# First sweep of a bidirectional GLA + latent-attention layer: chunk products in float32 from whole operands, the two directions' scores on the two halves of the rows

## The chip, the cores and the metric

The kernel runs on one core of a Trainium2 chip. Its time is the device time of one execution in microseconds. Three runs of the kernel before took 1295.48, 1295.50 and 1295.51 us; the median is 1295.5 us.

The engines of the core are named as in the profile: PE multiplies matrices (PEld is its loading of the stationary operand, "the weights"), DVE, ACT and POOL work elementwise, SP issues DMAs. PE writes to PSUM only.

## What is computed

One encoder layer on 2048 tokens of width 1024: one input projection, two groups of mixers beside each other (gated linear attention, GLA, and latent softmax attention, MLA), one output projection, LayerNorm. The change lies in the GLA alone, for which the reference does this, once forwards and once backwards over the sequence (in chunks of 64; four heads, keys of width 64, values of width 128):

```python
b = jnp.cumsum(gc, axis=3)              # running log decay inside a chunk
q_dec = qc * jnp.exp(b)
k_dec = kc * jnp.exp(-b)
k_tail = kc * jnp.exp(b_last - b)
attn = jnp.where(mask, jnp.einsum('nbhtd,nbhsd->nbhts', q_dec, k_dec), 0.0)
o_intra = jnp.einsum('nbhts,nbhsv->nbhtv', attn, vc)
def step(state, inp):
    qd, kt, vv, bl = inp
    o = jnp.einsum('bhtd,bhdv->bhtv', qd, state)
    state = state * jnp.exp(bl[:, :, 0, :])[..., None] + jnp.einsum('bhsd,bhsv->bhdv', kt, vv)
    return state, o
```

All of it is float32.

## The kernel before

**Two sweeps and an attention.** The sequence is cut into 16 chunks of 128 tokens. The first sweep (`sweep_a`) goes through them from the last (c = 15, i = 0) to the first (c = 0, i = 15). For each it projects x onto the GLA columns (`products`: three groups of columns, tile `ipa`) and the gate (`gate_products`, tile `ipg`), forms the decays (`ga_z`, `ga_sums`), and computes the chunk's own part of the GLA in both directions plus the running state of the backward direction. The second sweep (`sweep_c`) goes forwards, reads what the first has stored to DRAM, and makes the keys and queries of the MLA; then come the attention and the output.

**Both directions in one tile.** The 128 partitions of `qd` and `kd` hold 64 key dimensions of the forward direction and, below them, 64 of the backward direction. So a head's scores are two products over 64 rows each: rows 0 to 63 give the forward scores, rows 64 to 127 the backward ones.

**Split products.** Products that need more than one pass of precision are made from high and low parts in the type float32r: `hi` (L370, a copy on ACT into float32r) and `lo` (L376, the difference, on DVE or POOL). `mm3` (L424 to L426) is high x high, high x low, low x high. In the first sweep this is done for

- the scores `Ap` (`ga_intra`): `kd` is split into `kh` and `kl`; `qd` is split into `qbh` and `qbl`, which are laid out block-diagonally (`[P, H, 2, P]`, zeros outside the blocks, set once by POOL at the start), so that one product of 128 rows gives both directions, 256 columns wide. Twelve products for a chunk;
- the state's update `Up` (`ga_state`): `kd` transposed, split into `kth`, `ktl`, against `VV`, which holds the values' high and low part beside each other. A 256-column product and a 128-column one for each head: eight;
- the output of the chunk `Op` (`ga_av`): the masked scores `At` split into `Ah`, `Al`, against `VV`. Eight.

Results that are 256 columns wide hold two halves that ACT and DVE then add: `Us` (ACT copy L1047, DVE add L1049, scaled by the decay `cw` on POOL at L1051) and `oi` (L1029, L1031).

**Order.** Chunks 15 to 12 (i = 0 to 3) follow the string `ORDER_A`, whose entries name a step of a generator (`ga_q`, `ga_k`, ...; a step ends at a `yield`); `in_order` ties the instructions of each engine to this order. From i = 4 the steps of a chunk are placed between the products of the next one by `STEPS_A`: `intra` after the last products of group 1, `state` after the fourth k-step of group 2, `av` in the gate's products. Within this the framework's scheduler orders each engine's instructions. PE works through them in order.

**State.** `Sb` (rows 64 to 127) is the backward state. `ga_bst` stores `Sb` times one decay and multiplies `Sb` by another (POOL, L1072 and L1076); the last step of `ga_state` adds `Us` (POOL, L1057). From i = 3 `ga_bst` runs inside `ga_state`; before that `ORDER_A` places it.

**Buffers.** `gp` is a PSUM pool of two buffers of two banks each, used in turn by `Ap`, `Up`, `Op`. `g1` and `wa` hold the sweep's tiles in SBUF; when the sweep ends the weights of the second sweep (`wm`, `wz`) are loaded where the first sweep's were.

Of the kernel before, what the change touches and what calls it, by code (L numbers as in the profile page):

```python
# [18 lines left out]
P = 128  # L19
# [4 lines left out]
H = 4  # L24
# [58 lines left out]
    lo=(11.99, 11.22, 11.21, 12.62, 11.98, 11.51, 10.87, 10.63),  # L83
    pv=(12.35, 12.1, 11.89, 12.65, 12.27, 12.25, 12.14, 11.45),
# [20 lines left out]
    lo=(15.35, 16.07, 20.38, 20.41, 24.45, 25.82, 33.5, 36.25),  # L105
    pv=(16.29, 16.53, 21.45, 24.62, 26.22, 30.32, 41.89, 43.83),
# [82 lines left out]
    lo=(-0.5, 0.357),  # L189
# [79 lines left out]
    lo=(-0.452, -1.813),  # L269
# [65 lines left out]
    lo=(-0.124, 0.045),  # L335
# [24 lines left out]
class K:  # L360
# [262 lines left out]
    def sweep_a(self):  # L623
        tc, nc, ins, cp = self.tc, self.nc, self.ins, self.cp
        with ExitStack() as ctx:
            wp = ctx.enter_context(tc.tile_pool(name="wa", bufs=1, reuse_waits="tile"))
            xp, ip, tr, gp = self.xab, self.ip, self.tr, self.gp
# [3 lines left out]
            mask = wp.tile([P, P], I32, name="mask")  # L631
            rmask = wp.tile([P, H, P], F32, name="rmask")
            wg = wp.tile([98, H, P], F32R, name="wg")
            lrs = [wp.tile([P, 98], F32R, name=f"lr{i}") for i in range(2)]
            qbh = [wp.tile([P, H, 2, P], F32R, name=f"qbh{i}") for i in range(1)]
            qbl = [wp.tile([P, H, 2, P], F32R, name=f"qbl{i}") for i in range(1)]
            Sb = wp.tile([P, H, P], F32, name="Sb")
            pos_i = wp.tile([P, NCH], I32, name="pos_i")
            pos_f = wp.tile([P, NCH], F32, name="pos_f")
# [4 lines left out]
            nc.scalar.preload_act_table_set(EXP_LN)  # L644
            for t in lrs:
                nc.vector.memset(t[:, 96:98].bitcast(F32), 1.0)
            for t in qbh + qbl:
                nc.gpsimd.memset(t.bitcast(F32), 0.0)
            nc.vector.memset(Sb, 0.0)

            with tc.tile_pool(name="sta", bufs=1, reuse_waits="tile") as sta:
# [5 lines left out]
                for g, (_, n) in enumerate(A_GROUPS):  # L657
                    k = 0
                    for m in W_PIECES[g]:
# [26 lines left out]
            nc.sync.dma_start(invf, ins["invf"])  # L686
            g1 = ctx.enter_context(tc.tile_pool(name="g1", bufs=1))

            cst = dict(qbh=qbh[0], qbl=qbl[0], Sb=Sb, mask=mask, rmask=rmask, wg=wg, g1=g1, tr=tr, gp=gp)
            rope = self.rope_angles(pos_i, pos_f, invf, hpi)  # L690
            ch = self.ch = [dict(cst, c=NCH - 1 - i, i=i, lr=lrs[i % 2]) for i in range(NCH)]
            self.wa = [(wah[:, k], wal[:, k]) for k in range(NK)]
# [26 lines left out]
            for t in ORDER_A.split():  # L719
                n, i = t.split(".")  # L720
# [6 lines left out]
            for i in range(4, NCH):  # L727
                c = ch[i]["c"]
# [13 lines left out]
            i = NCH - 1  # L742
# [5 lines left out]
                    run("kt", i)  # L748
            self.xlate.append(self.split_x(self.xab, self.xraw, NCH - 2, "xb", "dve", 2))
            run("intra", i)  # L750
            with self.after(ch[i]["Ahi"]):
                self.gate_end(0, g1)
            run("state", i)
            run("av", i)
# [46 lines left out]
        yield  # L801

    def ga_v1(self, d):
        VV = d["VV"] = d["g1"].tile([P, H, 2, P], F32R, tag="VV", name=f"VV_{d['c']}", bufs=2)
        self.hi(VV[:, 0, 0], d["pt", 1][:, 256:384])
        yield
        self.lo(VV[:, 0, 1], d["pt", 1][:, 256:384], VV[:, 0, 0])
        yield

    def ga_v3(self, d):  # L810
        VV, pv = d["VV"], d["pt", 2][:, 0:384].rearrange("p (h d) -> p h d", h=3)
        self.hi(VV[:, 1:4, 0], pv)
        yield
        self.lo(VV[:, 1:4, 1], pv, VV[:, 1:4, 0])
        yield

    def ga_ld(self, i):
# [131 lines left out]
    def ga_q(self, d):  # L949

        nc, c = self.nc, d["c"]
        qbh, qbl = d["qbh"], d["qbl"]
        qT = d["tr"].tile([P, H, P], F32, tag="tr", name=f"qT{c}")
        for h in range(H):
            nc.tensor.transpose(qT[:, h], d["q2"][:, h].rearrange("p a d -> p (a d)"), self.ident)
        yield
        qd = self.t512(d, "qd")
        nc.vector.scalar_tensor_tensor(qd, qT, 0.125, d["E1"], ALU.mult, ALU.mult)
        self.store(c).dma_start(self.qd_s[c], qd.rearrange("p h t -> p (h t)"))
        yield  # L960
        halves = (slice(0, 64), 0), (slice(64, 128), 1)
        for r, j in halves:
            self.hi(qbh[r, :, j], qd[r])
            yield
        for r, j in halves:
            self.lo(qbl[r, :, j], qd[r], qbh[r, :, j])
            yield

    def ga_k(self, d):

        nc, c = self.nc, d["c"]
        kT = d["tr"].tile([P, H, P], F32, tag="tr", name=f"kT{c}")
        for h in range(H):
            nc.tensor.transpose(kT[:, h], d["k2"][:, h].rearrange("p a d -> p (a d)"), self.ident)
        yield
        kd = d["kd"] = self.t512(d, "kd")
        nc.vector.tensor_tensor(kd, kT, d["E2"], ALU.mult)
        yield
        kh = d["kh"] = self.t512(d, "kh", dt=F32R)
        self.hi(kh, kd)  # L980
        yield
        kl = d["kl"] = self.t512(d, "kl", dt=F32R)
        self.lo(kl, kd, kh)
        yield

    def ga_kt(self, d):

        nc, c = self.nc, d["c"]
        kt = d["tr"].tile([P, H, P], F32, tag="tr", name=f"kt{c}")
        for h in range(H):  # L990
            nc.tensor.transpose(kt[:, h], d["kd"][:, h], self.ident)
        yield
        kth = d["kth"] = self.t512(d, "kth", dt=F32R)
        self.hi(kth, kt)
        yield
        ktl = d["ktl"] = self.t512(d, "ktl", dt=F32R)
        self.lo(ktl, kt, kth)
        yield

    def ga_intra(self, d):  # L1000

        nc, c = self.nc, d["c"]
        Ap = d["gp"].tile([P, H, 2, P], F32, tag="gp", name=f"Ap{c}")
        for h in range(H):
            self.mm3(Ap[:, h], d["kh"][:, h], d["kl"][:, h], d["qbh"][:, h], d["qbl"][:, h])
        yield
        At = self.t512(d, "At")
        nc.scalar.activation(At, Ap[:, :, 1], AF.Copy)
        yield
        nc.vector.copy_predicated(At, d["mask"][:, None, :].to_broadcast([P, H, P]), Ap[:, :, 0])  # L1010
        yield
        Ah = d["Ah"] = self.t512(d, "Ah", dt=F32R)
        d["Ahi"] = self.hi(Ah, At)
        yield
        Al = d["Al"] = self.t512(d, "Al", dt=F32R)
        self.lo(Al, At, Ah)
        yield

    def ga_av(self, d):
        nc, c = self.nc, d["c"]  # L1020
        mm = nc.tensor.matmul
        Ah, Al, VV = d["Ah"], d["Al"], d["VV"]
        Op = d["gp"].tile([P, H, 2, P], F32, tag="gp", name=f"Op{c}")
        for h in range(H):
            mm(Op[:, h], Ah[:, h], VV[:, h], start=True, stop=False)
            mm(Op[:, h, 0], Al[:, h], VV[:, h, 0], start=False, stop=True)
        yield
        oi = self.t512(d, "oi", bufs=2)
        nc.scalar.activation(oi, Op[:, :, 1], AF.Copy)  # L1029
        yield  # L1030
        nc.vector.tensor_tensor(oi, Op[:, :, 0], oi, ALU.add)  # L1031
        self.store(c).dma_start(self.oi_s[c], oi.rearrange("p h t -> p (h t)"))
        yield

    def ga_state(self, d):

        nc, c = self.nc, d["c"]
        mm, V, G = nc.tensor.matmul, nc.vector, nc.gpsimd
        kth, ktl, VV, Sb, cw = d["kth"], d["ktl"], d["VV"], d["Sb"], self.cw[:, c]
        lo, up = slice(0, 64), slice(64, 128)  # L1040
        Up = d["gp"].tile([P, H, 2, P], F32, tag="gp", name=f"Up{c}")
        for h in range(H):
            mm(Up[:, h], kth[:, h], VV[:, h], start=True, stop=False)
            mm(Up[:, h, 0], ktl[:, h], VV[:, h, 0], start=False, stop=True)
        yield
        Us = self.t512(d, "Us")
        nc.scalar.activation(Us, Up[:, :, 1], AF.Copy)  # L1047
        yield
        V.tensor_tensor(Us, Up[:, :, 0], Us, ALU.add)  # L1049
        yield  # L1050
        G.tensor_tensor(Us, Us, cw[:, 1, :, None].to_broadcast([P, H, P]), ALU.mult)  # L1051
        self.store(c).dma_start(self.su_s[c][lo], Us.rearrange("p h t -> p (h t)")[lo])
        yield
        if d["i"] > 2:
            yield from self.ga_bst(d)
        if c > 0:
            G.tensor_tensor(Sb[up], Sb[up], Us[up], ALU.add)  # L1057
        yield

    def ga_bst(self, d):  # L1060
# [987 lines left out]
```

## Time and profile before

| | |
|---|---|
| median of three runs | 1295.5 us |
| the profiled execution, its time | 1295.28 us |
| its span, first to last instruction | 1293.4 us |
| mean granted TensorE clock | 0.998 |
| busy over the span: PE, PEld | 1273.7 us, 1127.9 us |
| busy over the span: DVE, ACT, POOL | 962.8, 816.2, 786.1 us |
| DMA | 145.81 MB, mean 113 GB/s |

The profile times each instruction in one execution. The difference between the profiled time and its span, 1.9 us, lies outside the instructions. A PE row gives the time from the start of a product to its modelled end; products overlap in the pipeline, so what a product costs in a stream is the distance from its start to the start of the next. The first sweep's products end at about 358 us; two late gates of chunks 15 and 14 follow up to about 367 us.

### The profile page before, as it was taken

The page shows a single profiled execution, that of the slowest core. Times are in us where ns is not written, and L with a number is a line of the kernel's source. Part 1 is how long each engine was busy: PE and PEld are TensorE (multiplying, and loading weights), DVE is VectorE, ACT ScalarE, POOL GpSimd, SP SyncE. Part 2 cuts the span into 40 slices and gives each one's busy share as a digit, 9 for nine tenths or more (in the row PEclk, how much of TensorE's full clock was granted, in tenths as well). Part 3 has the DMA queues.
Part 4 walks back from the last instruction along what each step waited for, and adds up shares of the span by engine and source line. Part 5 has one row for each costly group of instructions (what it writes and reads, how often), then busy time and mean ns, then how long its engine had stood idle before and what let it go on. Part 6 is the DMA issues. An engine that isn't in the chain of part 4 may idle for free.

```text
span 1293.4 us, 19959 instructions
## 1 busy us (share of the span) xinstructions
PE 1273.7 (98%) x7082; PEld 1127.9 (87%) x7082; DVE 962.8 (74%) x1706; ACT 816.2 (63%) x1334; POOL 786.1 (61%) x494
## 2 busy tenths in 40 slices
PE   8999999999999999999999999999999999999997
PEld 7999999999989999999788888888888888888886
DVE  7966675656675455554898888888888889469997
ACT  7765656566676656665688888888888888511110
POOL 0143333242458666762298888889999999944441
PEclk9999999999999999999999999999999999999999
DMA  8222313132475555665401111122223110366652
GB/s 294 66 92 56 93 53 94 50 86 62 143 261 174 194 197 179 200 208 174 128 1 41 42 42 41 42 58 63 61 72 103 46 41 9 123 214 201 214 193 98
DMA packets 105795, 145.81 MB, mean 113 GB/s; under 512 B 16630, under 2 KB 59262, under 8 KB 105696
## 3 DMA queue, kind: packets, MB, share of 16 engines
q1 hardware_dynamic: 97632, 142.41, 35.3%
q0 software_dynamic: 672, 2.10, 0.4%
q8 instruction: 56, 0.92, 0.3%
q10 hardware_dynamic: 7392, 0.03, 0.3%
q14 instruction: 43, 0.35, 0.1%
HBM read 94.14 MB, written 50.36 MB: 112 GB/s over the span
## 4 chain that ended last, share of the span: by engine, by line
PE 85%; DVE 4%; issue 2%; POOL 2%; ACT 1%; DMA 1%; SPq 0%; DVEq 0%; POOLq 0%
PE pz L1222 6%; PE ipm L1293 5%; PE o L424 4%; PE o L425 4%; PE o L426 4%; PE pS L1554 4%; PE pS L1556 4%; PE pS L1557 4%; PE pS L1555 4%; PE pS L1558 4%; PE ipa L424 4%; PE ipa L426 4%; PE ipa L425 4%; PE ipg L424 2%; PE ipg L425 2%
## 5 line engine op out<-in xcount | busy, mean ns | idle before, releaser
L376 POOL TENSOR_TENSOR pl<-s,ph 128x1024 fp32r<-128x1024 f32 x128 | 306.1, 2409 | 57.5 <-ACT ph L370 53.6
L1576 DVE TENSOR_TENSOR rm<-pS,rm 128x512 f32<-128x512 f32 x210 | 144.8, 690 | 35.8 <-ACT s L1563 30.5
L1563 ACT ACTIVATE s<-pS 128x1024 f32<-128x1024 f32 x128 | 131.3, 1026 | 61.0 <-PE pS L1558 50.8
L1600 DVE TENSOR_TENSOR s<-s,mb 128x1024 f32<-128x1024 f32 x128 | 151.2, 1213 | 9.2 <-PE mb L1594 9.0
L1051 POOL TENSOR_TENSOR Us<-Us,cw 128x512 f32<-128x512 f32 x16 | 20.0, 1247 | 226.3 <-DVE Us L1049 187.8
L370 ACT ACTIVATE ph<-s 128x1024 fp32r<-128x1024 f32 x128 | 135.1, 1057 | 17.4 <-PE o L426 16.6
L1604 ACT ACTIVATE s<-s 128x1024 f32<-128x1024 f32 x128 | 131.4, 1050 | 11.9 <-DVE s L1600 11.9
L424 PE MATMUL ipa<-wah,xah 128*128 128x384 f32 (+1 forms) x384 | 129.0, 336 | 5.4 <-ACT wah L370 5.4
L425 PE MATMUL ipa<-wal,xah 128*128 128x384 f32 (+1 forms) x384 | 124.3, 324 | 0.6 <-DVE wal L376 0.5
L426 PE MATMUL ipa<-wah,xal 128*128 128x384 f32 (+1 forms) x384 | 124.4, 324 | 0.0
L1554 PE MATMUL pS<-qh,ckvT_h 128*128 128x512 f32 x256 | 102.6, 401 | 0.8 <-DVE rm L1576 0.4
L424 PE MATMUL o<-ph,vh 128*128 128x512 f32 x256 | 101.0, 395 | 0.0
L426 PE MATMUL o<-ph,vl 128*128 128x512 f32 x256 | 99.8, 390 | 0.0
L1556 PE MATMUL pS<-qh,ckvT_l 128*128 128x512 f32 x256 | 99.8, 390 | 0.0
L1557 PE MATMUL pS<-rh,krs 128*128 128x512 f32 x256 | 99.8, 390 | 0.0
L1558 PE MATMUL pS<-rl,krs 128*128 128x512 f32 x256 | 99.7, 389 | 0.0
L1555 PE MATMUL pS<-ql,ckvT_h 128*128 128x512 f32 x256 | 99.7, 389 | 0.0
L425 PE MATMUL o<-pl,vh 128*128 128x512 f32 x256 | 99.7, 389 | 0.0
L1627 DVE TENSOR_TENSOR ap<-ap,s 128x512 f32<-128x512 f32 x120 | 83.1, 692 | 2.6 <-ACT s L1604 0.7
L376 POOL TENSOR_TENSOR ol<-of,oh 128x512 fp32r<-128x512 f32 x32 | 42.9, 1342 | 63.8 <-ACT oh L370 63.8
L424 PEld LDWEIGHTS ipa<-wah,xah 128*128 128x128 f32 x384 | 72.8, 190 | 6.6 <-ACT wah L370 5.6
L425 PEld LDWEIGHTS ipa<-wal,xah 128*128 128x128 f32 x384 | 72.8, 190 | 1.8 <-DVE wal L376 1.3
(325 smaller groups left out, 3838.8 us busy)
## 6 DMA issues: line engine op xcount, KB each, us to landing
xcf<-xT_dram SPq DMA_DIRECT2D x16, 512.0 KB, 5.6
xr<-x_dram SPq DMA_DIRECT2D x16, 512.0 KB, 5.5
out_dram<-rr SPq DMA_DIRECT2D x32, 256.0 KB, 2.1
xaf<-xT_dram SPq DMA_DIRECT2D x14, 512.0 KB, 4.2
oib<-oi_s SPq DMA_DIRECT2D x16, 256.0 KB, 4.3
qdb<-qd_s SPq DMA_DIRECT2D x16, 256.0 KB, 5.1
SU<-su_s SPq DMA_DIRECT2D x16, 256.0 KB, 4.9
ub<-u_s SPq DMA_DIRECT2D x16, 256.0 KB, 4.2
```

The costliest lines, as they stand in the source:

```text
L370: return nc.scalar.activation(dst, src, AF.Copy).ins
L376: return e.tensor_tensor(dst, src, hi.bitcast(F32), ALU.subtract).ins
L424: mm(out, ah, bh, start=start, stop=False)
L425: mm(out, ah, bl, start=False, stop=False)
L426: mm(out, al, bh, start=False, stop=stop)
L1554: mm(ps[:, e], kh, qh, start=True, stop=False)
L1555: mm(ps[:, e], kh, ql, start=False, stop=False)
L1556: mm(ps[:, e], kl, qh, start=False, stop=False)
L1557: mm(ps[:, e], kr, rh, start=False, stop=False)
L1558: mm(ps[:, e], kr, rl, start=False, stop=True)
L1576: V.tensor_tensor(d["rm"], src[:, e], d["rm"], ALU.max)
L1600: V.tensor_tensor(s, s, d["mb"][:, None, :].to_broadcast([P, 2, QB]), ALU.subtract)
```

## The change

All three kinds of product are made from whole float32 tiles instead of high and low parts.

- `ga_q` and `ga_k` end with `qd` and `kd`; the tiles `qbh`, `qbl`, `kh`, `kl` and the two memsets go.
- `ga_kt` and `ga_v1`/`ga_v3` copy `kt` and `V` out of PSUM once, on ACT (the copies that were the high parts), as float32; the low parts go.
- `ga_intra`: eight products a chunk, each of 64 rows by 128 columns. The two directions of a head take turns, rows 0 to 63 and rows 64 to 127, and write to different banks of PSUM (`Ap` is now `[P, 2, H, P]`). The masking is as before; `Ah` and `Al` go.
- `ga_av` and `ga_state`: four products of 128 by 128 each. `oi` is one ACT copy; `Us` is one DVE product out of PSUM with the decay `cw`, in place of an ACT copy, a DVE add and a POOL product, and its store to `su_s` is issued behind it. The empty `yield`s keep the state's addition in the fifth step of `ga_state`, behind `ga_bst`.
- `gate_end` of the last chunk waits for the masked scores (`Aset`) instead of their high part (`Ahi`).

On PE the order of the work stays as it was, but for one chunk (i = 4, in which the previous chunk's `kt` transposes and one of its eight score products come before the products of group 1), the place of one `lrT` transpose, and the last chunk, whose `Op` products are no longer spread among those of the late gate.

```diff
-            qbh = [wp.tile([P, H, 2, P], F32R, name=f"qbh{i}") for i in range(1)]
-            qbl = [wp.tile([P, H, 2, P], F32R, name=f"qbl{i}") for i in range(1)]
...
-            for t in qbh + qbl:
-                nc.gpsimd.memset(t.bitcast(F32), 0.0)
...
-            with self.after(ch[i]["Ahi"]):
+            with self.after(ch[i]["Aset"]):
                 self.gate_end(0, g1)
...
     def ga_v1(self, d):
-        VV = d["VV"] = d["g1"].tile([P, H, 2, P], F32R, tag="VV", name=f"VV_{d['c']}", bufs=2)
-        self.hi(VV[:, 0, 0], d["pt", 1][:, 256:384])
-        yield
-        self.lo(VV[:, 0, 1], d["pt", 1][:, 256:384], VV[:, 0, 0])
+        d["V"] = self.t512(d, "V", bufs=2)
+        self.hi(d["V"][:, 0], d["pt", 1][:, 256:384])
         yield
...
     def ga_q(self, d):
...
-        for r, j in halves:
-            self.hi(qbh[r, :, j], qd[r])
-            yield
-        for r, j in halves:
-            self.lo(qbl[r, :, j], qd[r], qbh[r, :, j])
-            yield
...
     def ga_k(self, d):
...
-        kh = d["kh"] = self.t512(d, "kh", dt=F32R)
-        self.hi(kh, kd)
-        yield
-        kl = d["kl"] = self.t512(d, "kl", dt=F32R)
-        self.lo(kl, kd, kh)
-        yield
...
     def ga_kt(self, d):
...
-        kth = d["kth"] = self.t512(d, "kth", dt=F32R)
-        self.hi(kth, kt)
-        yield
-        ktl = d["ktl"] = self.t512(d, "ktl", dt=F32R)
-        self.lo(ktl, kt, kth)
+        d["kt"] = self.t512(d, "kt")
+        self.hi(d["kt"], kt)
         yield
...
     def ga_intra(self, d):
-        Ap = d["gp"].tile([P, H, 2, P], F32, tag="gp", name=f"Ap{c}")
+        Ap = d["gp"].tile([P, 2, H, P], F32, tag="gp", name=f"Ap{c}")
         for h in range(H):
-            self.mm3(Ap[:, h], d["kh"][:, h], d["kl"][:, h], d["qbh"][:, h], d["qbl"][:, h])
-        yield
...
-        Ah = d["Ah"] = self.t512(d, "Ah", dt=F32R)
-        d["Ahi"] = self.hi(Ah, At)
-        yield
-        Al = d["Al"] = self.t512(d, "Al", dt=F32R)
-        self.lo(Al, At, Ah)
+            for j, r in enumerate((slice(0, 64), slice(64, 128))):
+                nc.tensor.matmul(Ap[:, j, h], d["kd"][r, h], d["qd"][r, h], start=True, stop=True)
+        yield
+        At = d["At"] = self.t512(d, "At")
+        nc.scalar.activation(At, Ap[:, 1], AF.Copy)
+        yield
+        d["Aset"] = nc.vector.copy_predicated(At, d["mask"][:, None, :].to_broadcast([P, H, P]), Ap[:, 0]).ins
         yield
...
     def ga_av(self, d):
-            mm(Op[:, h], Ah[:, h], VV[:, h], start=True, stop=False)
-            mm(Op[:, h, 0], Al[:, h], VV[:, h, 0], start=False, stop=True)
+            nc.tensor.matmul(Op[:, h], d["At"][:, h], d["V"][:, h], start=True, stop=True)
         yield
         oi = self.t512(d, "oi", bufs=2)
-        nc.scalar.activation(oi, Op[:, :, 1], AF.Copy)
-        yield
-        nc.vector.tensor_tensor(oi, Op[:, :, 0], oi, ALU.add)
+        nc.scalar.activation(oi, Op, AF.Copy)
...
     def ga_state(self, d):
-            mm(Up[:, h], kth[:, h], VV[:, h], start=True, stop=False)
-            mm(Up[:, h, 0], ktl[:, h], VV[:, h, 0], start=False, stop=True)
+            nc.tensor.matmul(Up[:, h], d["kt"][:, h], d["V"][:, h], start=True, stop=True)
         yield
         Us = self.t512(d, "Us")
-        nc.scalar.activation(Us, Up[:, :, 1], AF.Copy)
-        yield
-        V.tensor_tensor(Us, Up[:, :, 0], Us, ALU.add)
-        yield
-        G.tensor_tensor(Us, Us, cw[:, 1, :, None].to_broadcast([P, H, P]), ALU.mult)
+        nc.vector.tensor_tensor(Us, Up, cw[:, 1, :, None].to_broadcast([P, H, P]), ALU.mult)
         self.store(c).dma_start(self.su_s[c][lo], Us.rearrange("p h t -> p (h t)")[lo])
+        yield
+        yield
         yield
         if d["i"] > 2:
             yield from self.ga_bst(d)
         if c > 0:
-            G.tensor_tensor(Sb[up], Sb[up], Us[up], ALU.add)
+            nc.gpsimd.tensor_tensor(Sb[up], Sb[up], Us[up], ALU.add)
```

More of the change, by code (lines that the diff above doesn't have):

```diff
@@ L687, in sweep_a @@
             g1 = ctx.enter_context(tc.tile_pool(name="g1", bufs=1))
-            cst = dict(qbh=qbh[0], qbl=qbl[0], Sb=Sb, mask=mask, rmask=rmask, wg=wg, g1=g1, tr=tr, gp=gp)
+            cst = dict(Sb=Sb, mask=mask, rmask=rmask, wg=wg, g1=g1, tr=tr, gp=gp)
             rope = self.rope_angles(pos_i, pos_f, invf, hpi)
@@ L803, in ga_v1 @@
     def ga_v1(self, d):
-        VV = d["VV"] = d["g1"].tile([P, H, 2, P], F32R, tag="VV", name=f"VV_{d['c']}", bufs=2)
-        self.hi(VV[:, 0, 0], d["pt", 1][:, 256:384])
-        yield
-        self.lo(VV[:, 0, 1], d["pt", 1][:, 256:384], VV[:, 0, 0])
+        d["V"] = self.t512(d, "V", bufs=2)
+        self.hi(d["V"][:, 0], d["pt", 1][:, 256:384])
         yield
     def ga_v3(self, d):
-        VV, pv = d["VV"], d["pt", 2][:, 0:384].rearrange("p (h d) -> p h d", h=3)
-        self.hi(VV[:, 1:4, 0], pv)
-        yield
-        self.lo(VV[:, 1:4, 1], pv, VV[:, 1:4, 0])
+        self.hi(d["V"][:, 1:4], d["pt", 2][:, 0:384].rearrange("p (h d) -> p h d", h=3))
         yield
@@ L951, in ga_q @@
         nc, c = self.nc, d["c"]
-        qbh, qbl = d["qbh"], d["qbl"]
         qT = d["tr"].tile([P, H, P], F32, tag="tr", name=f"qT{c}")
@@ L956, in ga_q @@
         yield
-        qd = self.t512(d, "qd")
+        qd = d["qd"] = self.t512(d, "qd")
         nc.vector.scalar_tensor_tensor(qd, qT, 0.125, d["E1"], ALU.mult, ALU.mult)
@@ L960, in ga_q @@
         yield
-        halves = (slice(0, 64), 0), (slice(64, 128), 1)
-        for r, j in halves:
-            self.hi(qbh[r, :, j], qd[r])
-            yield
-        for r, j in halves:
-            self.lo(qbl[r, :, j], qd[r], qbh[r, :, j])
-            yield
     def ga_k(self, d):
@@ L1002, in ga_intra @@
         nc, c = self.nc, d["c"]
-        Ap = d["gp"].tile([P, H, 2, P], F32, tag="gp", name=f"Ap{c}")
+        Ap = d["gp"].tile([P, 2, H, P], F32, tag="gp", name=f"Ap{c}")
         for h in range(H):
-            self.mm3(Ap[:, h], d["kh"][:, h], d["kl"][:, h], d["qbh"][:, h], d["qbl"][:, h])
+            for j, r in enumerate((slice(0, 64), slice(64, 128))):
+                nc.tensor.matmul(Ap[:, j, h], d["kd"][r, h], d["qd"][r, h], start=True, stop=True)
         yield
-        At = self.t512(d, "At")
-        nc.scalar.activation(At, Ap[:, :, 1], AF.Copy)
+        At = d["At"] = self.t512(d, "At")
+        nc.scalar.activation(At, Ap[:, 1], AF.Copy)
         yield
-        nc.vector.copy_predicated(At, d["mask"][:, None, :].to_broadcast([P, H, P]), Ap[:, :, 0])
-        yield
-        Ah = d["Ah"] = self.t512(d, "Ah", dt=F32R)
-        d["Ahi"] = self.hi(Ah, At)
-        yield
-        Al = d["Al"] = self.t512(d, "Al", dt=F32R)
-        self.lo(Al, At, Ah)
+        d["Aset"] = nc.vector.copy_predicated(At, d["mask"][:, None, :].to_broadcast([P, H, P]), Ap[:, 0]).ins
         yield
@@ L1020, in ga_av @@
         nc, c = self.nc, d["c"]
-        mm = nc.tensor.matmul
-        Ah, Al, VV = d["Ah"], d["Al"], d["VV"]
-        Op = d["gp"].tile([P, H, 2, P], F32, tag="gp", name=f"Op{c}")
+        Op = d["gp"].tile([P, 2, H, P], F32, tag="gp", name=f"Op{c}")[:, 0]
         for h in range(H):
-            mm(Op[:, h], Ah[:, h], VV[:, h], start=True, stop=False)
-            mm(Op[:, h, 0], Al[:, h], VV[:, h, 0], start=False, stop=True)
+            nc.tensor.matmul(Op[:, h], d["At"][:, h], d["V"][:, h], start=True, stop=True)
         yield
         oi = self.t512(d, "oi", bufs=2)
-        nc.scalar.activation(oi, Op[:, :, 1], AF.Copy)
-        yield
-        nc.vector.tensor_tensor(oi, Op[:, :, 0], oi, ALU.add)
+        nc.scalar.activation(oi, Op, AF.Copy)
         self.store(c).dma_start(self.oi_s[c], oi.rearrange("p h t -> p (h t)"))
@@ L1037, in ga_state @@
         nc, c = self.nc, d["c"]
-        mm, V, G = nc.tensor.matmul, nc.vector, nc.gpsimd
-        kth, ktl, VV, Sb, cw = d["kth"], d["ktl"], d["VV"], d["Sb"], self.cw[:, c]
+        Sb, cw = d["Sb"], self.cw[:, c]
         lo, up = slice(0, 64), slice(64, 128)
-        Up = d["gp"].tile([P, H, 2, P], F32, tag="gp", name=f"Up{c}")
+        Up = d["gp"].tile([P, 2, H, P], F32, tag="gp", name=f"Up{c}")[:, 0]
         for h in range(H):
-            mm(Up[:, h], kth[:, h], VV[:, h], start=True, stop=False)
-            mm(Up[:, h, 0], ktl[:, h], VV[:, h, 0], start=False, stop=True)
+            nc.tensor.matmul(Up[:, h], d["kt"][:, h], d["V"][:, h], start=True, stop=True)
         yield
         Us = self.t512(d, "Us")
-        nc.scalar.activation(Us, Up[:, :, 1], AF.Copy)
+        nc.vector.tensor_tensor(Us, Up, cw[:, 1, :, None].to_broadcast([P, H, P]), ALU.mult)
+        self.store(c).dma_start(self.su_s[c][lo], Us.rearrange("p h t -> p (h t)")[lo])
         yield
-        V.tensor_tensor(Us, Up[:, :, 0], Us, ALU.add)
         yield
-        G.tensor_tensor(Us, Us, cw[:, 1, :, None].to_broadcast([P, H, P]), ALU.mult)
-        self.store(c).dma_start(self.su_s[c][lo], Us.rearrange("p h t -> p (h t)")[lo])
         yield
```

## The prediction

> **What bounds the kernel now.** I read the page first, then the busy times of the first sweep against the rest, then the timeline of PE in one chunk, then the list of waits.
>
> ```profile
> span 1293.4 us, 19959 instructions
> PE 1273.7 (98%) x7082; PEld 1127.9 (87%) x7082; DVE 962.8 (74%) x1706; ACT 816.2 (63%) x1334; POOL 786.1 (61%) x494
> PEclk9999999999999999999999999999999999999999
> PE 85%; DVE 4%; issue 2%; POOL 2%; ACT 1%; DMA 1%; SPq 0%; DVEq 0%; POOLq 0%
> 0.00:365.00 365.00, 357.38 (x2245) 337.58 (x2246) 248.37 (x434) 229.72 (x442) 112.86 (x89) 1.00 0.34 107
> 81.50:345.00 263.50, 263.16 (x1677) 250.60 (x1676) 166.72 (x303) 158.68 (x303) 86.90 (x61) 1.00 0.25 72
> ```
>
> The last two rows are stretches of the span: PE, PEld, DVE, ACT, POOL busy, then the granted clock. PE is busy for 263.16 of the 263.50 us in which the first sweep runs in its steady order, at full clock; DVE for 166.72, ACT for 158.68. The chain of work that ended last is 85% PE. So in the stage that the change touches, time is what PE needs for its list of products, plus the few moments in which it waits. Work taken off DVE, ACT and POOL is worth only those moments. What a product costs is the distance between starts, here in the last but one chunk:
>
> ```profile
> 338.17 0.28 PE L424 MATMUL Ap<-qbh,kh 128*128 128x256 f32 x1
> ...
> 339.58 0.34 PE L424 MATMUL ipa<-wah,xah 128*128 128x384 f32 x1
> ...
> 341.67 0.28 PE L1043 MATMUL Up<-VV,kth 128*128 128x256 f32 x1
> ...
> 341.79 0.22 PE L1044 MATMUL Up<-VV,ktl 128*128 128x128 f32 x1
> 341.79 0.19 PEld L1043 LDWEIGHTS Up<-VV,kth 128*128 128x128 f32 x1
> 341.85 0.33 PE L1043 MATMUL Up<-VV,kth 128*128 128x256 f32 x1
> 341.90 0.19 PEld L1044 LDWEIGHTS Up<-VV,ktl 128*128 128x128 f32 x1
> ...
> 342.54 0.39 PE L424 MATMUL ipa<-wah,xah 128*128 128x384 f32 x1
> ...
> 345.48 0.37 PE L1025 MATMUL Op<-VV,Ah 128*128 128x256 f32 x1
> ...
> 346.44 0.44 PE L424 MATMUL ipg<-wgh,xah 128*128 128x512 f32 x1
> ```
>
> The twelve products of `Ap` take 339.58 - 338.17 = 1.41 us, the eight of `Up` 0.87, the eight of `Op` 0.96. A 256-column and a 128-column product cost about the same on average, because weights are loaded every 0.11 us (341.79, 341.90) whatever is streamed behind them.
>
> **The change part by part.** 28 float32r products a chunk, 1.41 + 0.87 + 0.96 = 3.24 us, become 16 float32 products: eight of 64 rows, eight of 128. The one full float32 product of before that isn't a transpose is `pabs`, eight products of 128 by 128 in the second sweep's setup:
>
> ```profile
> 372.23 1.96 PEld L1186 LDWEIGHTS pabs<-wkr,wqT 128*128 128x128 f32 x16
> 372.43 1.95 PE L1186 MATMUL pabs<-wkr,wqT 128*128 128x128 f32 x16
> 374.10 0.19 PEld L1222 LDWEIGHTS pz<-xch,wzh 128*128 128x128 f32 x1
> 374.13 0.36 PE L1222 MATMUL pz<-xch,wzh 128*128 128x256 f32 x1
> ```
>
> Eight products leave 16 records: each is run as two weight loads and two passes. By the starts of the passes a record costs (374.13 - 372.43) / 16 = 0.106 us, by those of the loads (374.10 - 372.23) / 16 = 0.117 us. I take 0.11.
>
> *`Up` and `Op`*: 8 products, 16 records, 1.76 us against 1.83, so -0.07 us a chunk, -1.1 us in 16 chunks. With 0.106 it is -2.1, with 0.117 it is +0.7. Half as many products, but each is loaded twice: next to nothing.
>
> *`Ap`*: 8 products, 16 records. No row of the trace shows a product on half of the rows, so its price is bounded from both sides. If the halves go one after the other, it is the `pabs` price: 1.76 us, +0.35 against 1.41, +5.6 us in 16 chunks (+4.6 with 0.106, +7.4 with 0.117). If the two halves go side by side, the second pass of one runs with the first of the other, and 16 records fill 9 places: 0.99 us, -0.42 a chunk, -6.7 us (9 x 0.117: -5.7; 8 places of 0.106: -9.0). I take side by side. In the built program the two halves alternate, use different rows and write different banks. Two facts of the rows above are near to it: products can start 0.06 us apart (341.79 and 341.85), so issuing doesn't hold them at 0.11, and a load lasts 0.19 and the next begins after 0.11, so two loads are under way at once already where they share their rows. That is no proof for two halves, and the other bound stays as a rival. The Trainium skill, "TensorEngine Tiling (Array Packing)", section "Tiling Modes", says that tiles of the array load weights and multiply independently; no run here shows it yet.
>
> *Entering and leaving the halves.* Twice a chunk PE goes between products over 128 rows and over 64 (one chunk has one `Ap` product apart: one more pair). The only change of the array's division in the trace is `rt`, which the built program puts on a 128x32 part of the array:
>
> ```profile
> 1185.59 0.27 PE L1681 MATMUL rt<-ident,rc 128*4 128x128 f32 x1 [0.24 <-DVE rc L1669]
> 1185.61 0.48 PE L424 MATMUL po<-woh,oh 128*128 128x512 f32 x1
> 1185.93 0.39 PE L425 MATMUL po<-wol,oh 128*128 128x512 f32 x1
> 1186.16 0.39 PE L426 MATMUL po<-woh,ol 128*128 128x512 f32 x1
> ```
>
> From `rt` to the second `po` pass 0.34 us: 0.11 for `rt` and 0.23 for a 512-column product (1185.93 to 1186.16). Leaving costs nothing there; entering can't be seen, as PE was waiting for DVE. I take 0. The upper bound is a full stop: an `Ap` row is 0.28 long and uses 0.12 of it (1.41 / 12), so 0.16 to empty, and a load of 0.11 before the next product, 0.27 each, 32 times: +8.7 us. The same page of the skill, section "Tiling Modes", says that changing the mode drains the engine; the `rt` rows disagree on leaving (0.34, where the drain would make it 0.61), and by the rule the sum would be 8.7 us higher.
>
> *Waits of PE that the split parts cause.*
>
> ```profile
> PEld Op L1025 <- ACT Ah L370: 0.9, 1, 0.9
> PEld Up L1044 <- DVE ktl L376: 0.7, 1, 0.7
> PEld Ap L426 <- DVE kl L376: 0.5, 1, 0.5
> PE Up L1044 <- DVE ktl L376: 0.4, 1, 0.4
> PE Op L1025 <- ACT Ah L370: 0.4, 1, 0.4
> PE Ap L426 <- DVE kl L376: 0.3, 1, 0.3
> ```
>
> (us in all, times, longest.) The producers `Ah`, `ktl`, `kl` are gone. By PE's idle 1.1 us are to be had, by the loads 2.1. What is then last is the masked `At`, `kt` and `kd`, each one or two instructions earlier in the same chain. I take -1.5.
>
> *Off PE.* A chunk loses on DVE two `qbl`, `kl`, `ktl`, `Al`, two low parts of the values and an add; on ACT two `qbh`, `kh`, `Ah` and the copy of `Us`; on POOL one product. All of it lies beside PE, which the rows above show full: nothing. The stores are as many as before (`qd_s`, `oi_s`, two halves of `su_s`); the lower half of `su_s` goes out behind a DVE instruction instead of a POOL one, so sooner, and on SP's queue it changes places with a few neighbours in the first four chunks; on POOL's queue, in the last two, it and `qd_s` come a little later in the order. Nobody reads them before the second sweep: nothing.
>
> *The new wait.* `Us` on DVE now waits for `Up` itself, which was ACT's wait:
>
> ```profile
> ACT Us L1047 <- PE Up L1044: 3.5, 12, 0.6
> DVE qd L958 <- PE qT L955: 38.8, 11, 3.9
> ```
>
> Behind it on DVE stand the scans of the decays and then `qd`, for which PE's scores wait. DVE idles 38.8 / 11 = 3.5 us a chunk before `qd` alone, and a wait is 0.6 at most: hidden. Without that cover it costs 0.6 a chunk, 9.6 us.
>
> *Sum.* -6.7 - 1.1 + 0 - 1.5 = -9.3 us on the profiled 1295.28 us (its span of 1293.4 and 1.9 around it; 0.2 under the median of the runs shown): 1286.0 us. The extremes of this case: -9.0 - 2.1 - 2.1 = -13.2, 1282.1 us, and -5.7 + 0.7 - 1.1 = -6.1, 1289.2 us.
>
> **The rivals.**
>
> *The halves go in turn (slower).* Place: the eight score products; price +5.6 in place of -6.7; it decides as soon as the second half's weights can't be loaded while the first half's are. Sum +5.6 - 1.1 - 1.5 = +3.0: 1298.3 us (1295.7 to 1302.3 by the bounds of the terms). For it: the rows show a load every 0.11 us in all three groups, and no two products that go on together. Against it: the two facts given above.
>
> *PE stops at every change between 128 and 64 rows.* +8.7 on either: 1294.7 us with the halves side by side, 1307.0 in turn. Against it the `rt` rows; for it, that entering has no row.
>
> *DVE takes ACT's wait and passes it on to the scores.* +9.6 on the forecast: 1295.6 us, no change. Against it the 3.5 us of idle time, which grow by the eight instructions that DVE loses.
>
> **How the numbers follow.** Chances: forecast 0.49; in turn 0.28; stops 0.17 (0.07 side by side, 0.10 in turn); DVE 0.06. A run of this kernel tells 0.2%, 2.6 us, from no change, so "same" is 1292.9 to 1298.1. The forecast is wholly faster. In turn: 0.10 same, 0.18 slower. Stops side by side: 0.02 faster, 0.03 same, 0.02 slower; stops in turn: slower. DVE: 0.03 same, 0.03 slower. Faster 0.51, same 0.16, slower 0.33. The range runs from the forecast's lower end, 1282, to 1300.5, which takes in the larger part of "in turn" and leaves out its top and the stops in turn, less than 0.2 together. The forecast's own range is 1282 to 1289.
>
> **What will show it.** In the changed profile: the distance from the first of eight consecutive `Ap` products to the next `ipa` product, 1.0 us side by side, 1.8 in turn; the distance from the last `Ap` to that `ipa` product, 0.11 without a stop and up to 0.38 with one; `Up` and `Op` at about 0.88 us each; the six waits above gone, and none on `Us` or `qd` before PE in their place; no change in the length of anything behind the first sweep. Wrong would be the whole argument if PE is no longer full in the steady stretch, and its main term if consecutive `Ap` records start 0.11 us apart throughout.

## The result and the profile after

The changed kernel takes 1293.68 us (median of 20 runs, 1292.97 to 1295.17) against 1295.98 us of the kernel before in the same job. The ratio is 0.9982, 95% interval 0.9975 to 0.9989: 2.3 us faster, where 9.3 were forecast. The interval leaves out 1, so there is a gain, but it is less than the 2.6 us that the prediction took as the least to be told from no change.

The page of the changed kernel: its span, the busy time of the engines, and the head of the chain that ended last.

```profile
span 1292.6 us, 19828 instructions
PE 1273.0 (98%) x7146; PEld 1123.5 (87%) x7146; DVE 886.4 (69%) x1578; ACT 768.3 (59%) x1254; POOL 763.2 (59%) x476
PE 88%; DMA 4%; DVE 3%; POOL 2%; issue 2%; ACT 1%; SPq 0%; DVEq 0%; POOLq 0%
```

DVE, ACT and POOL lost 76, 48 and 23 us of work, and the span shrank by 0.8. PE is as full as before. The chain now has 4% of DMA, where it had 1%; its two largest pieces lie between the sweeps, a store of `oi` (8.1 us from 348.53) and the load of `qdb` behind it (6.5 us). This execution of the changed kernel also began late: its first product of the second chunk began at 23.04 us against 21.73 before. In the profiles of the experiments e1, e2, e3 and e7, which do the same work as the changed kernel up to that point, it began at 21.6 to 22.4, so about 1 us of the difference between the two spans is likely chance, and the median of the runs is the better measure.

To see where time went I cut each profile at two products. From the first product of the second chunk to the first `ipm` product, which belongs to the second sweep, the kernel before takes 367.56 - 21.73 = 345.83 us and the changed one 365.14 - 23.04 = 342.10, so the changed sweep gains 3.7 us. From the first `ipm` product to the last it is 223.03 us before and 224.55 after: the second sweep, whose products are the same, loses 1.5. Behind that nothing differs by more than 0.2 us.

Now the timeline of PE at the score products of the last but one chunk.

```profile
336.00 0.33 PE L426 MATMUL ipa<-wah,xal 128*128 128x384 f32 x1
336.26 0.97 PEld L980 LDWEIGHTS Ap<-qd,kd 64*128 64x128 f32 x16 [0.25 <-issue]
336.26 1.16 PE L980 MATMUL Ap<-qd,kd 64*128 64x128 f32 x16
337.35 0.19 PEld L424 LDWEIGHTS ipa<-wah,xah 128*128 128x128 f32 x1
337.35 0.44 PE L424 MATMUL ipa<-wah,xah 128*128 128x384 f32 x1
...
337.63 0.34 PE L425 MATMUL ipa<-wal,xah 128*128 128x384 f32 x1
337.63 0.19 PEld L426 LDWEIGHTS ipa<-wah,xal 128*128 128x128 f32 x1
337.81 0.35 PE L426 MATMUL ipa<-wah,xal 128*128 128x384 f32 x1
```

To price a group of products, I take the time from the start of the `ipa` product ahead of it to the start of the second one behind it, less two ordinary `ipa` products of 0.175 us. That counts what the group does to its neighbours too. Here it is 337.63 - 336.00 - 0.35 = 1.28 us. By the rows shown before the same group cost 1.41 us. So the scores gain 0.13 us in this chunk. In eleven of the sixteen chunks the `z` products of the gate, not an `ipa` product, stand ahead of the scores. There I take the time from the start of `z` to the start of the second `ipa` product, first in the changed kernel, then before:

```profile
313.64 0.56 PE L894 MATMUL z<-lrTs,wg 98*128 98x128 f32 x4
314.13 1.16 PE L980 MATMUL Ap<-qd,kd 64*128 64x128 f32 x16
...
315.50 0.33 PE L425 MATMUL ipa<-wal,xah 128*128 128x384 f32 x1
```

```profile
315.51 0.56 PE L903 MATMUL z<-lrTs,wg 98*128 98x128 f32 x4
...
317.56 0.34 PE L425 MATMUL ipa<-wal,xah 128*128 128x384 f32 x1
```

315.50 - 313.64 = 1.86 us against 317.56 - 315.51 = 2.05: here the gain is 0.19 us.

Inside the group the halves do go side by side: the 16 passes end 1.16 us after the first start, and the last of them is 0.27 long, so all starts lie within 0.89 us. That is 0.10 for the first load and 7 steps of 0.11: eight pairs, not sixteen single passes. What eats the gain stands at the two ends. The first load of `Ap` starts 0.26 us after the last `ipa` product, although loads elsewhere begin with the product ahead of them (337.63), and the profile names no other engine for it: "issue". Behind the group the first `ipa` load starts at 337.35, 0.20 us after the last pass of `Ap` (337.15 = 336.26 + 1.16 - 0.27), and its product is 0.44 long in place of 0.34, since it waits for that load.

All 17 score groups of the trace look like this. The first load of `Ap` starts 0.20 us after the start of the last product ahead where that has 128 columns (`z`, `kt`), 0.22 with 288 columns, 0.26 with 384 and 0.32 with 512 (`ipg`); behind the group it is 0.20 us every time. In all 34 places the load starts 0.07 us before the modelled end of the product ahead. So at each of these changes between whole and half rows PE starts to load only when the product under way is nearly through.

The state's product, by the same measure, costs 340.63 - 339.39 - 0.35 = 0.89 us, 0.02 less than the 0.91 of the kernel before; `Op` gains 0.02 as well:

```profile
339.39 0.34 PE L426 MATMUL ipa<-wah,xal 128*128 128x384 f32 x1
...
339.57 1.05 PE L1006 MATMUL Up<-V,kt 128*128 128x128 f32 x8
...
340.37 0.42 PE L424 MATMUL ipa<-wah,xah 128*128 128x384 f32 x1
...
340.63 0.33 PE L425 MATMUL ipa<-wal,xah 128*128 128x384 f32 x1
```

Of the list of waits (us in all, times, longest), the lines in which PE waits for the new parts:

```profile
PEld Ap L980 <- issue: 1.5, 6, 0.4
PEld ipm L1253 <- DVE xcl L376: 1.2, 1, 1.2
PE ipm L1253 <- DVE xcl L376: 0.8, 1, 0.8
PE Op L992 <- DVE At L985: 0.6, 1, 0.6
```

The six waits on split parts are gone, but the last chunk's `Op` now waits 0.6 us for the masked scores themselves, and at the start of the second sweep PE waits for `xcl`, which DVE makes. The timeline of DVE there shows why it is late:

```profile
356.21 3.49 DVE L376 TENSOR_TENSOR wml<-wmr,wmh 128x448 fp32r<-128x448 f32 x5 [1.18 <-ACT wmh L370]
362.27 0.48 DVE L1083 MEMSET Sf<- 64x512 f32 x1 [2.57 <-DMA oi_s<-oi]
362.68 2.65 DVE L376 TENSOR_TENSOR wml<-wmr,wmh 128x448 fp32r<-128x448 f32 x3
365.25 2.36 DVE L376 TENSOR_TENSOR xcl<-xcf,xch 128x1024 fp32r<-128x1024 f32 x2
```

The memset that clears the second sweep's state stands two instructions earlier in DVE's order than before (after five of the eight `wml`, where it was after seven), and waits 2.57 us for the DMA that stores the first sweep's last `oi`. Three `wml` and both `xcl` queue behind it. The wait itself is new too. Before, the memset ran while that store was still under way: the store was issued at 360.60 and landed 4.8 us later, at 365.4.

```profile
360.60 0.54 POOL L1032 DMA_DIRECT2D oi_s<-oi  x1
```

```profile
364.71 0.48 DVE L1123 MEMSET Sf<- 64x512 f32 x1
```

So in the changed kernel the memset depends on a store that it did not depend on before. That `Sf` now lies in memory that `oi` had would explain it; the traces hold no addresses, so this is not shown.

### The profile page after: what moved, and what is told of

Read it like the earlier page. It is cut to its first block, busy times and chain, and to the rows that moved or that the text cites. A ratio compares the mean times of both kernels' runs of the same rounds, so it can differ in the third digit from the quotient of the medians.

```text
span 1292.6 us, 19828 instructions
## 1 busy us (share of the span) xinstructions
PE 1273.0 (98%) x7146; PEld 1123.5 (87%) x7146; DVE 886.4 (69%) x1578; ACT 768.3 (59%) x1254; POOL 763.2 (59%) x476
## 4 chain that ended last, share of the span: by engine, by line
PE 88%; DMA 4%; DVE 3%; POOL 2%; issue 2%; ACT 1%; SPq 0%; DVEq 0%; POOLq 0%
PE pz L1182 6%; PE ipa L424 5%; PE ipm L1253 5%; PE ipa L425 5%; PE ipa L426 5%; PE o L424 4%; PE o L425 4%; PE o L426 4%; PE pS L1514 4%; PE pS L1516 4%; PE pS L1517 4%; PE pS L1515 4%; PE pS L1518 4%; PE ipg L426 2%; PE ipg L424 2%; PE ipg L425 2%
## 5 line engine op out<-in xcount | busy, mean ns | idle before, releaser
L424 PE MATMUL ipa<-wah,xah 128*128 128x384 f32 (+1 forms) x384 | 132.7, 346 | 5.9 <-ACT wah L370 5.9
L1017 POOL TENSOR_TENSOR Sb<-Sb,Us 64x512 f32<-64x512 f32 x15 | 20.8, 1386 | 194.1 <-ACT E L931 138.7
```

The source lines that it names most:

```text
L424: mm(out, ah, bh, start=start, stop=False)
```

## The experiments

Two things had to be told apart: whether the time at the two ends of the score group is PE's own stop or a wait for something, and what the memset costs. Medians and ratios are against the kernel before in the same job (medians 1295.67 and 1295.68 us there, 0.3 below the job of the changed kernel). Each experiment has 5 to 11 runs; differences between two of them are known to about 1 us, and to about 1.5 us for e4 and e7.

**e1, score products over all rows.** The scores are left out: the values' tile is multiplied with itself in their place.

```diff
-            for j, r in enumerate((slice(0, 64), slice(64, 128))):
-                nc.tensor.matmul(Ap[:, j, h], d["kd"][r, h], d["qd"][r, h], start=True, stop=True)
+            nc.tensor.matmul(Ap[:, 0, h], d["V"][:, h], d["V"][:, h], start=True, stop=True)
...
-        nc.scalar.activation(At, Ap[:, 1], AF.Copy)
+        nc.scalar.activation(At, Ap[:, 0], AF.Copy)
```

> The changed kernel with the score products taken over 128 rows: four products a chunk of the values' tile with itself in place of the eight half-row ones, so the scores, and with them the GLA output, are not the reference's; everything behind them stays. Theory A (PE stops each time it goes between 128-row and 64-row products, 0.2 us on entering and 0.2 on leaving; the halves themselves go side by side at 0.11 us a pair of passes): four products take as long as eight half-row ones, 0.9 us, and the stops go, 0.39 us in each of 16 chunks: -6.2 us against the changed kernel, about 1287.5 us. Theory B (the time before and after the half-row products is a wait for their inputs or for their PSUM buffer): the gaps stay, at most -1 us, 1293 us.

Measured 1287.81 us, ratio 0.9940 (0.9928 to 0.9953). PE's timeline at the same place:

```profile
329.89 0.34 PE L426 MATMUL ipa<-wah,xal 128*128 128x384 f32 x1
329.90 1.04 PEld L979 LDWEIGHTS Ap<-V 128*128 128x128 f32 x8
330.07 1.05 PE L979 MATMUL Ap<-V 128*128 128x128 f32 x8
...
330.88 0.42 PE L424 MATMUL ipa<-wah,xah 128*128 128x384 f32 x1
...
331.14 0.34 PE L425 MATMUL ipa<-wal,xah 128*128 128x384 f32 x1
```

The first load begins with the product ahead of it (329.90 against 329.89), and the group costs 331.14 - 329.89 - 0.35 = 0.90 us, 0.38 less than the half rows. Behind `z` it is 0.35 less:

```profile
307.89 0.56 PE L894 MATMUL z<-lrTs,wg 98*128 98x128 f32 x4
...
309.40 0.33 PE L425 MATMUL ipa<-wal,xah 128*128 128x384 f32 x1
```

309.40 - 307.89 = 1.51 us against 1.86. Eleven groups stand behind `z` and six behind other products: 11 x 0.35 + 6 x 0.38 = 6.1 us; the runs show 5.9. That fits the stops. It doesn't rule out a wait for `qd` or `kd`, which this kernel doesn't read here; e4 and e7 do.

**e2, the halves in turn.** The loops over `j` and `h` are exchanged.

> The changed kernel with the same eight half-row products in another order: the four of rows 0 to 63 first, then the four of rows 64 to 127. Theory A (two neighbouring products on different halves run side by side): only the pair in the middle overlaps, 15 to 16 places of 0.11 us in place of 8, +0.8 us a chunk, +13 us, 1306.5 us. Theory B (a pass over 64 rows simply takes half as long, 0.056 us, whichever half it is on): no change, 1293.7 us.

Measured 1302.17 us, ratio 1.0048 (1.0036 to 1.0061): 8.5 us slower than the changed kernel, not 13.

```profile
343.01 0.34 PE L426 MATMUL ipa<-wah,xal 128*128 128x384 f32 x1
343.28 1.52 PEld L980 LDWEIGHTS Ap<-qd,kd 64*128 64x128 f32 x16 [0.25 <-issue]
343.28 1.71 PE L980 MATMUL Ap<-qd,kd 64*128 64x128 f32 x16
344.92 0.19 PEld L424 LDWEIGHTS ipa<-wah,xah 128*128 128x128 f32 x1
...
345.20 0.34 PE L425 MATMUL ipa<-wal,xah 128*128 128x384 f32 x1
```

The group costs 345.20 - 343.01 - 0.35 = 1.84 us. The starts span 1.71 - 0.27 = 1.44 us, five steps of 0.11 more than with the halves alternating. So a pass over 64 rows is not simply half as long: it is the neighbourhood of the other half that makes the pair cheap. Theory A's size was off: 16 passes in 13 places, because three passes of the second half run beside the last of the first. The 0.25 us of "issue" at entry are the same as with the other order.

**e3, the memset on POOL.**

```diff
-            self.nc.vector.memset(Sf, 0.0)
+            self.nc.gpsimd.memset(Sf, 0.0)
```

> The changed kernel with the zeroing of the second sweep's state (Sf) issued by POOL instead of DVE. Theory A (in the changed kernel this memset stands two instructions earlier on DVE and waits 2.57 us there for the DMA that stores the last oi, and the splits of the second sweep's weights behind it come late): the 0.97 us wait of PE at the first ipm product and part of the 0.32 at pz go, -1.0 to -1.6 us, 1292.4 us. Theory B (the x or weight loads set the start of the second sweep, and the memset waits beside them): 0, 1293.7 us.

Measured 1291.34 us, ratio 0.9967 (0.9955 to 0.9979): 2.3 us less than the changed kernel, more than expected. DVE goes through all eight `wml` without the gap, and PE through `ipm`:

```profile
355.33 5.64 DVE L376 TENSOR_TENSOR wml<-wmr,wmh 128x448 fp32r<-128x448 f32 x8 [1.18 <-ACT wmh L370]
360.89 1.22 DVE L376 TENSOR_TENSOR xcl<-xcf,xch 128x1024 fp32r<-128x1024 f32 x1
```

```profile
364.47 0.37 PE L1253 MATMUL ipm<-wml,xch 128*128 128x448 f32 x1
364.68 0.36 PE L1253 MATMUL ipm<-wmh,xcl 128*128 128x448 f32 x1
```

`xcl` starts at 360.89 in place of 365.25, and its first `ipm` product 0.21 us behind the one ahead. In the changed kernel that distance was over a microsecond:

```profile
365.34 0.37 PE L1253 MATMUL ipm<-wml,xch 128*128 128x448 f32 x1
366.52 0.47 PE L1253 MATMUL ipm<-wmh,xcl 128*128 128x448 f32 x1 [0.81 <-DVE xcl L376]
```

On POOL the memset stands behind the store in the queue and in front of nothing that is urgent. Of the 2.3 us 1.0 are lost at this place; the rest comes in the first steps of the second sweep, whose other weights DVE splits behind `xcl`. At the first `ipm` product e3 is 0.9 us ahead of the changed kernel's profile (its earlier start), at the last 3.5.

**e9, the same edit in the kernel before.**

> The kernel before with its one memset of Sf on POOL instead of DVE. Theory A (the memset costs in the changed kernel because of its place on DVE and the store that it waits for; in the kernel before it waited for nothing): 0 to -0.5 us, 1295.5 us. Theory B (the memset on DVE costs in either kernel, and e3's gain has nothing to do with the change): -2.3 us, 1293.4 us.

Measured 1296.27 us, ratio 1.0004 (0.9995 to 1.0013): nothing that the noise lets one see. So the memset is a cost of the changed kernel alone, as its wait is.

**e4, one more pair of changes between 64 and 128 rows.** Beside e3, heads 0 and 1 are issued a step earlier than heads 2 and 3 in twelve chunks.

```diff
-        for h in range(H):
-            for j, r in enumerate((slice(0, 64), slice(64, 128))):
-                nc.tensor.matmul(Ap[:, j, h], d["kd"][r, h], d["qd"][r, h], start=True, stop=True)
+        for h in range(H) if "Ap" not in d else (2, 3):
+            self.score(d, h)
...
+    def ga_in0(self, d):
+        self.score(d, 0)
+        self.score(d, 1)
...
-STEPS_A = {(0, 4): [("q", "prev"), ("k", "prev")], (1, 4): [("kt", "prev"), ("lrT", "cur")],
+STEPS_A = {(0, 4): [("q", "prev"), ("k", "prev")], (1, 4): [("kt", "prev"), ("lrT", "cur")], (1, 6): [("in0", "prev")],
...
```

> As e3 (the changed kernel, memset on POOL), with the eight score products of a chunk issued in two groups of four, two products' worth of projection apart, in the twelve chunks that follow the fixed steps: the same work, one more entering and leaving of the half rows in each. Theory A (0.39 us a pair of changes): 12 x 0.39 = +4.7 us against e3, 1296.0 us. Theory B (gaps are waits for inputs or buffers): 0, 1291.3 us.

Measured 1295.92 us, ratio 1.0001 (0.9992 to 1.0010): 4.6 us more than e3, where theory A says 4.7. The first of the two groups in one chunk, and the start of the second:

```profile
337.57 0.34 PE L426 MATMUL ipa<-wah,xal 128*128 128x384 f32 x1
337.84 0.72 PE L991 MATMUL Ap<-qd,kd 64*128 64x128 f32 x8
338.48 0.45 PE L424 MATMUL ipa<-wah,xah 128*128 128x384 f32 x1
338.77 0.34 PE L425 MATMUL ipa<-wal,xah 128*128 128x384 f32 x1
...
339.92 0.33 PE L426 MATMUL ipa<-wah,xal 128*128 128x384 f32 x1
340.18 0.71 PE L991 MATMUL Ap<-qd,kd 64*128 64x128 f32 x8
```

338.77 - 337.57 - 0.35 = 0.85 us for half of the work that takes 1.28 in one group: 0.45 for four pairs and 0.40 that don't depend on their number. The second group reads tiles that the first had read and writes the buffer that the first had begun, and yet it starts 0.26 us behind the product ahead: no wait for an input or a buffer explains that.

**e7, two chunks' scores in one group.** Beside e3, from i = 4 on the scores and the output products of two chunks are issued together; `qd`, `kd`, `At` have two buffers and `V` three.

```diff
-                        run(n, i if d == "cur" else i - 1)
+                        if n in ("intra", "av"):
+                            for j in (i - 2, i - 1) if i % 2 else ():
+                                run(n, j)
+                        else:
+                            run(n, i if d == "cur" else i - 1)
...
+            run("av", i - 2)
             run("av", i - 1)
```

> The changed kernel with the memset on POOL, and from i = 4 on the score products (and the output products) of two chunks issued together every second chunk, with a second buffer for qd, kd and At and a third for V: 10 groups of half-row products in place of 16. Theory A (stops of 0.39 us a group): 6 x 0.39 = -2.3 us beside the memset's -1.0 to -1.6, about 1290 us. Theory B (the gaps are waits for inputs or buffers): the memset's part alone or less, 1292.4 us or more, as two groups now queue for the two PSUM buffers.

Measured 1289.52 us, ratio 0.9951 (0.9938 to 0.9963), the fastest kernel of this study that computes the layer: 6.2 us under the kernel before, 1.8 under e3.

```profile
330.14 0.33 PE L426 MATMUL ipa<-wah,xal 128*128 128x384 f32 x1
330.41 2.06 PE L985 MATMUL Ap<-qd,kd 64*128 64x128 f32 x32
332.39 0.44 PE L424 MATMUL ipa<-wah,xah 128*128 128x384 f32 x1
332.67 0.34 PE L425 MATMUL ipa<-wal,xah 128*128 128x384 f32 x1
```

Two chunks cost 332.67 - 330.14 - 0.35 = 2.18 us in place of 2.56: one pair of stops of 0.38 less. The trace has 10 groups in place of 17, since the extra one at i = 4 goes too, and 7 x 0.35 to 0.38 is 2.5 to 2.7 us. The first sweep is indeed 2.7 us shorter than in e3 (339.53 against 342.26), but the second is 0.8 longer, for a reason that is not known; together that is near the 1.8 of the runs.

**e5 and e6, one half of the change at a time** (each beside e3). In e5 the scores are split float32r products again (`ga_q`, `ga_k` and the products of `ga_intra` as before), output and state stay float32; in e6 it is the other way round (`ga_v1`, `ga_v3`, `ga_kt`, `ga_av`, `ga_state` as before, with `Ah` and `Al`).

> As e3, with the scores alone put back to the split float32r form over 128 rows (twelve products, block-diagonal qbh and qbl, kh, kl); output and state products stay float32. Theory A: half rows and their stops 1.28 us against 1.41 us a chunk, so this is +0.13 x 16 = +2.0 us, and up to 1 us for waits on the split parts: 1293.3 to 1294.4 us. Theory B (the float32 scores bring nothing or lose, the gain is elsewhere): 1291.3 us or less.

Measured 1294.69 us, ratio 0.9992 (0.9983 to 1.0001), 3.35 us more than e3.

> As e3, with the output and state products alone put back to the split float32r form (VV, Ah, Al, kth, ktl, the adds, the POOL product for Us); scores stay half-row float32. Theory A: 16 products of 0.115 us against 16 passes of 0.11, +1.1 us in 16 chunks, and +0.5 to +1.5 us for PE's waits on Ah and ktl: 1293 to 1294 us. Theory B (DVE's direct Us out of PSUM delays the scores): this is faster than e3.

Measured 1292.54 us, ratio 0.9976 (0.9967 to 0.9985), 1.2 us more than e3.

The stretches of the profiles, one execution each, in us:

| | first product of chunk 2 to first `ipm` | first to last `ipm` |
|---|---|---|
| before | 345.83 | 223.03 |
| e9, memset on POOL | 345.85 | 222.75 |
| changed | 342.10 | 224.55 |
| e1, whole rows | 335.65 | 225.49 |
| e2, in turn | 350.32 | 224.50 |
| e3, memset on POOL | 342.26 | 221.91 |
| e4, one more pair of changes | 347.06 | 221.79 |
| e5, scores split | 345.29 | 222.47 |
| e6, output and state split | 342.13 | 223.03 |
| e7, two chunks | 339.53 | 222.75 |

So with the memset out of the way the half-row scores are worth 3.4 us, 3.0 of them in the first sweep. About 2.2 are the products. The rest fits waits that e5's trace lists: PE's loads wait 0.5 us for `kl`, 0.2 for `kh` and, in two places, 0.6 for `gs`, which DVE makes beside the split parts.

The output and state products are another matter. e6 goes through the first sweep in the same time as e3: the wait for `ktl` is back in its third chunk (24.90 us in place of 24.17) and the fourth takes 0.2 longer, but its chunk i = 4 has no extra pair of stops (22.27 in place of 22.68), and the rest is a little shorter. The 1.1 us by which its profile is longer lie in the second sweep, which e6 doesn't change, and why is not known. So no gain from these products themselves is shown.

## Why the prediction was wrong

The forecast was a sum of four terms, -6.7 - 1.1 + 0 - 1.5.

- *`Ap` side by side, -6.7.* The mechanism was right and the size too small: eight places, not nine, and starts within 0.89 us, 1.41 - 0.89 = 0.52 a chunk, -8.3 us (behind `z` 2.05 - 1.51 = 0.54 a chunk). The first passes of the two halves start together. e2 shows that the pairing is what makes it.
- *Entering and leaving the halves, 0.* This is the step that failed. "Leaving costs nothing there; entering can't be seen, as PE was waiting for DVE. I take 0." The stops are 0.35 us a pair of changes behind `z` and 0.38 to 0.40 behind other products (group ends of 1.28 - 0.89 here, the doubled group in e4, the saved ones in e7, their absence in e1), +6.1 us for 17 pairs. The forecast had bounded a pair at 0.54 and had made the full stop beside side-by-side halves a rival with 0.07, at 1294.7 us; that rival is what happened, at 0.7 of its price. The `rt` rows were read too far: `rt` has 4 columns and all 128 rows, and a cost seen to be nothing there was carried over to products on half of the rows. That the array is divided at all for `rt` is read from the built program; no row shows it. The rule of the Trainium skill, "TensorEngine Tiling (Array Packing)", section "Tiling Modes", that a change of mode drains the engine, agrees with every score group here, where the next load starts 0.07 us before the end of the product ahead; at `rt` the next load starts with `rt` itself (both at 1185.59), and why is open.
- *`Up` and `Op`, -1.1.* Not borne out. The two groups gained 0.02 us each, 0.05 a chunk where 0.07 were forecast, but PE loses 0.06 a chunk at the first product of the second column group (132.12 to the next start at 132.37; before, 132.27 to 132.47), which e6 does not. The cause of that is not shown. That e6's median is 1.2 us over e3, close to the forecast, is luck: its first sweep is as long as that of e3.
- *Waits of PE, -1.5.* Near. All six named waits went: from its first `ipa` product to that of the next chunk, the third chunk takes 24.17 us in place of 25.29, and the last but two 22.25 in place of 22.96, of which the scores' own gain is less than 0.2 each. In their place `Op` of the last chunk waits 0.6 us for `At`, one instruction up the same chain, which the forecast had named as next in line but not priced.
- *Off PE, nothing.* Wrong at one place that no term had: the memset of `Sf`, in front of three `wml` and `xcl` on DVE, began to wait for the store of `oi`. It costs about 2.3 us (e3), and nothing in the kernel before (e9). The forecast had counted the stores as unread until the second sweep, so that their time did not matter; but an instruction can wait for a store that it does not read.

Together: -8.3 + 6.1 for the scores, nothing for the other products and -1.5 of waits is -3.7 us, what the first sweep lost. With the 1.5 that the second sweep took more it is -2.2, against -2.3 of the medians. The agreement is closer than these terms are known. With the memset out of the way the gain is 4.3 us (e3), still less than half of the forecast: the stops are the larger miss.

Of the rivals, "in turn" fell (e2 is that case by construction, and slower), and "DVE takes ACT's wait" fell: the list of waits has no wait of the scores on `qd`.

## What to carry to other kernels

Two half-row products that alternate run at the price of one, but each change of PE between half and whole rows cost 0.2 us here: a group pays only if it is long, so collect such products (two chunks in a group gained 1.8 us more). A price read off one kind of change need not hold for another; where a row bounds a cost and nothing of the same kind has been seen, the middle of the bounds is a better guess than the friendly end. When tiles and instructions go, look at what the ones that stay now wait for, and at what stands behind them: the memset came to wait for a store, in front of urgent work. Price a group in more than one chunk: a gain of 0.13 us in the last but one chunk is 0.19 where `z` stands ahead.

## What was not expected of the hardware

- Two passes on different halves of the rows, each with its own weight load, take 0.11 us together, the same as one pass over 128 rows: eight pairs with their first load in 0.89 us of starts, and 32 passes with one entry in 2.06 us (e7).
- The entry and the exit cost about 0.2 us each and don't depend on how many products lie between (0.40 for four pairs, 0.39 for eight, and 2.18 - 16 x 0.11 = 0.4 for sixteen). They do depend on the product ahead: the first load waits 0.20 us behind a product of 128 columns and 0.32 behind one of 512. No such wait was seen behind `rt`, of 4 columns and 128 rows.
- With the halves in turn (e2) passes of the second half start before the first half is through: 13 places for 16 passes.
